# Small matmuls of two gated delta blocks woven into the weight products in a fixed order, and one parameter vector read as one row

## The chip, the cores and the metric

The kernel runs on one core of a Trainium2 chip. The metric is the device time of one execution in microseconds (us). TensorE (PE) multiplies, with its weight loads (PEld) overlapping; VectorE (DVE), ScalarE (ACT) and GpSimd (POOL) do elementwise work; SyncE (SP) and ACT issue the DMAs that matter here, each on a queue of its own.

## The reference

A four-layer hybrid model runs over a prompt of 256 tokens and eight samples of eight tokens, 320 rows of 1024 columns in all, in float32. Each layer is a half feed-forward, a mixer and another half feed-forward. The mixer is a gated delta rule (gdn) in layers 0 and 3, a chunked MLP in one, a state-space mixer (ssd) in one. The gdn mixer:

```python
def gdn_mixer(h, conv_buf, s0, w_in, conv_w, a_log, dt_bias, norm_w, w_out):
    qkv, gate, a_in, b_in = jnp.split(h @ w_in, ...)
    qkv, new_buf = causal_dwconv(qkv, conv_buf, conv_w)
    q, k, v = jnp.split(jax.nn.silu(qkv), [D_QK_A, 2 * D_QK_A], axis=-1)
    q, k = l2norm(q) * (DK_A ** -0.5), l2norm(k)
    g = -jnp.exp(a_log) * jax.nn.softplus(a_in + dt_bias)
    beta = jax.nn.sigmoid(b_in)
    o, s_new = gated_delta_chunked(q, k, v, g, beta, s0)
    o = rms_norm(o, norm_w) * jax.nn.silu(gate)
    return o @ w_out, (new_buf, s_new)
```

There are 8 heads of 128 columns. `gated_delta_chunked` works in chunks: a triangular 128x128 system per head and chunk, made of k·kᵀ, decays from the running sum of g, and beta, is inverted, and the chunk's outputs and the next state follow from it. The ssd mixer has a per-head skip weight, `ssd_d` (32 numbers), by which x is scaled and added to its output.

## The kernel before, in words

Activations stand transposed: 8 tiles of 128 features by 320 rows, each split in a high and a low part (`xhi`, `xlo`). Weights come from HBM in units of 512 KB (`raw`, L133, SP's queue), are split by ACT (`hi`, L134) and DVE (`lo`, L135), and each 128x128 weight block makes three matmuls of 320 columns (hi·hi, lo·hi, hi·lo; L160 to L162). These are called weight products below. The rest of a layer waits for little else than them.

In a gdn block (`gdn_core`, about 267 to 537 us and 2633 to 2903 us of the span) the input projection is done in pairs of heads: k, q, v and the gate g for four head pairs, 16 pairs of column blocks, each 48 weight products. Between and among them stand the chains, one for each head pair, over five 128x128 systems (two heads by two chunks, and the samples):

- `gdn_decay`: after the narrow a/b product, DVE works out softplus and g; PE makes running sums of g (L626 to L660), from which come the decays `Gm`.
- k, q, v pairs are evacuated (`cb`, L538, L539), convolved (one ACT row and three DVE taps, L546) and go through silu.
- `invert(q)`: U and Uq = k·kᵀ and k·qᵀ (L738), a DVE sequence to `L` (L763), a mask product (L768), a loop of 30 small GpSimd operations on `X` (L777, L778), `Dt` (L782), transposes (L786), and three levels of block products with copies between them (L792 to L824).
- `recur(q)`: solve (L860), products with the state (L853 to L868), the sample states (`across`, L898), the norm of the output (L910, L511 on GpSimd, L912), its transposes (L915), then the new sample states: matmuls (L933), DVE updates of `S` (L938), and a store to HBM (L940, SP's queue).

`GDN_ORDER` says between which parts of the chains each pair of products is written; a scheduler then sets the order on every engine by its own costs, with what is ready first. A matmul that waits holds those behind it on PE. `oT`, the gdn output, is split into `g_hi` (L335) and `g_lo` (L336) before the output projection; the memory that `g_hi` takes is free only when the last store of `S` has landed. `psm` is a PSUM pair for the weight products, `psx` and `psy` are sets of three for the chains.

The parameters of a mixer are fetched during the feed-forward before it (`prep_...`). `prep_ssd` reads `ssd_d` into `Dc` (128 partitions by 16), even heads in the upper 64 partitions, odd ones in the lower:

```python
Dc = p.tile([128, 16], F32, name="Dc")
for h in range(2):
    nc.scalar.dma_start(Dc[64 * h:64 * h + 64, :], d['ssd_d'][j].rearrange("(m h) -> h m", h=2)[h].partition_broadcast(64))
```

Of the kernel before, what the change touches and what calls it, by code (L numbers as in the profile page):

```python
# [15 lines left out]
KD = 8  # L16
# [59 lines left out]
GDN_ORDER = "k0 q0 v0,k1 q1,v1 k2,q2,v2,k3 q3,v3,g0,g2,g3 g1"  # L76
# [5 lines left out]
class Trunk:  # L82
    def __init__(self, tc, d, ctx):
# [14 lines left out]
        self.hold, self.homes = [], []  # L98
# [432 lines left out]
    def conv_tile(self, p, ps, ci, prm, cvo):  # L531

        nc = self.nc
        cb = p.tile([128, CB + 8], F32, tag="cb", name="cb", bufs=2)
# [7 lines left out]
                              cb[:, 256:355].rearrange("p (b c) -> p b c", c=11)[:, :, 0:3])  # L542
        y = p.tile([128, CB], F32, tag="cy", name="cy", bufs=2)
# [45 lines left out]
    def gdn_decay(self, t, ab, prep):  # L589
# [34 lines left out]
        g2 = g.rearrange("q p u -> q (p u)")  # L624
        ps, pg = self.psx(), self.psx()
# [47 lines left out]
        return beta, eG, neG, kdc, gt, gts, Gm, last, later  # L673
# [11 lines left out]
    def gdn_core(self, p, j, w_in, prep, cvo):  # L685
        nc, d = self.nc, self.d
        V, A, G, PE = nc.vector, nc.scalar, nc.gpsimd, nc.tensor
        mm = PE.matmul
# [12 lines left out]
        def project(kind, q):  # L701
            if kind == 'k':
# [3 lines left out]
            c0 = {'k': 1024, 'q': 0, 'v': 2048}[kind] + q * 256  # L706
            for h, ps in enumerate(self.pair(w_in, c0)):
                y = self.conv_tile(p, ps, c0 // 128 + h, prm, cvo)
                op, os_ = {'k': (kqp[h][:, :, 0, :], kqs[:, 0]), 'q': (kqp[h][:, :, 1, :], kqs[:, 1]), 'v': (vp[h], vs)}[kind]
                i = A.activation(op, y[:, :TP].rearrange("p (b n) -> p b n", b=2), AF.Silu)  # L710
                if q == 0 and kind != 'k':
                    self.behind(last, i)
                ys = y[:, 259:347].rearrange("p (k j c) -> p k j c", k=2, c=11)[:, :, :, 0:8]
                A.activation(self.rows(os_)[:, h], ys, AF.Silu)
                if kind != 'v':
                    A.activation(EE[q % 3][:, 'kq'.index(kind), 24:].rearrange("p (j k h t) -> p h k j t", j=4, k=2, h=2)[:, h, :, :, 0:8], ys, AF.Silu)

        def gate(q):
            for h, ps in enumerate(self.pair(w_in, 3072 + q * 256)):
                z = t([128, T], "zs", 2)  # L720
                V.tensor_tensor(z, ps, self.r, op=ALU.mult)
                if q in done:
                    A.activation(z, z, AF.Silu)
                    V.tensor_tensor(oT[:, 2 * q + h, :], oT[:, 2 * q + h, :], z, op=ALU.mult)
                else:
                    A.activation(oT[:, 2 * q + h, :], z, AF.Silu)
            gated.append(q)

        def invert(q, fill):
# [4 lines left out]
            U, Uq = t([128, 5, 128], "U"), t([128, 5, 128], "Uq", 2)  # L734
            for a, b in ((0, 2), (2, 4), (4, 5)):
# [25 lines left out]
            for lo, n, w in ((0, 8, 15), (8, 7, 7)):  # L761
# [3 lines left out]
                                d16[:, None, lo:lo + n, None].to_broadcast([128, 5, n, w]), op=ALU.mult)  # L765
            for a, b in ((0, 512), (512, 845)):
# [12 lines left out]
            for f, *a in fill:  # L779
                f(*a)  # L780
# [4 lines left out]
            for u in range(4):  # L785
                PE.transpose(ps[:, u * 128:(u + 1) * 128], Dt[:, u, :], self.ident)  # L786
            A.activation(Dn, ps.rearrange("p (u n) -> p u n", u=4), AF.Copy)
            for u0 in range(0, 4, 2):
                us = slice(u0, u0 + 2)
# [42 lines left out]

        def recur(q, kd, cc, sq, Uq, Dt, S):

            kqp, kqs, vp, vs = tiles.pop(q)
            qu = [kqp[0][:, 0, 1], kqp[0][:, 1, 1], kqp[1][:, 0, 1], kqp[1][:, 1, 1], kqs[:, 1]]
            vu = [vp[0][:, 0], vp[0][:, 1], vp[1][:, 0], vp[1][:, 1], vs]
            R, qss, oss, oe = t([128, 5, 128], "R"), t([128, 5], "qss", 2), t([128, 5], "oss", 2), t([128, 5], "oe", 2)
            for a, b in ((0, 4), (4, 5)):
                ps = self.psx()  # L840
                for u in range(a, b):
                    PE.transpose(ps[:, (u - a) * 128:(u - a + 1) * 128], vu[u], self.ident)
                for u in range(a, b):
                    A.activation(R[:, u], ps[:, (u - a) * 128:(u - a + 1) * 128], AF.Copy, scale=sq[:, u:u + 1])
            vn, o = t([128, 5, 128], "vn"), t([128, 5, 128], "o")
            Sp = t([128, 2, 128], "Sp")
            for b in range(2):
                if b == 1:
                    ps = self.psx()
                    for h in range(2):  # L850
                        for a in range(2):
                            c = (2 * h + a) * 128
                            mm(ps[:, c:c + 128], lhsT=kqp[h][:, 1, a, :], rhs=Sp[:, h], start=True, stop=True)  # L853
                    for h in range(2):
                        u = 2 * h + 1
                        V.scalar_tensor_tensor(R[:, u], ps[:, h * 256:h * 256 + 128], neG[:, q, u:u + 1], R[:, u], op0=ALU.mult, op1=ALU.add)
# [605 lines left out]
```

## Time and profile before

| | us |
|---|---|
| median of 3 runs | 3199.25 (3196.7 to 3200.08) |
| the profiled execution's own time | 3193.62 |
| span of the profiled execution | 3191.8 |
| PE busy, of the span | 3033.1 (95%) |
| DVE / ACT / POOL busy | 1965.6 / 1534.5 / 527.8 |
| mean granted PE clock | 0.966 |

The profiled execution is 5.6 us below the median of the runs. "Busy" is summed over the span; the granted clock is 1.00 where TensorE runs at 2.4 GHz and 0.50 where it runs at 1.2 GHz. Tile names in the rows are those of the program, `out<-in`; L and a number is a line of the kernel before.

### The profile page before, as it was taken

Reading aid. Unit: us, or ns where it says so; the run is one execution under the profiler, and the core shown is the slowest. Engines: PE = TensorE matmul, PEld = TensorE weight load, DVE = VectorE, ACT = ScalarE, POOL = GpSimd, SP = SyncE. Lnnn points to the kernel's source line nnn. Section 1 sums busy time; section 2 is a strip of 40 time slices with the busy share of each in tenths; the row PEclk is TensorE's granted clock in tenths of the full one; section 3 lists DMA queues with packets and bytes.
Section 4 is the critical chain, followed back from the end, with each engine's and each line's share of the span. In section 5 each row is a group of like instructions: output and inputs, shape, how many; then the busy total and the mean of one; then the engine's idle time right before and its main releaser. Section 6 shows DMA issues by size and latency. Waiting matters only on the chain.

```text
span 3191.8 us, 52917 instructions
## 1 busy us (share of the span) xinstructions
PE 3033.1 (95%) x20851; PEld 2907.4 (91%) x20851; DVE 1965.6 (62%) x3365; ACT 1534.5 (48%) x2739; POOL 527.8 (17%) x794
## 2 busy tenths in 40 slices
PE   8998899999999989999899888999999997999998
PEld 8998778999999989999899777799999997778998
DVE  5556775655655675664554787766646647766653
ACT  4445555544444535444444554454444445646443
POOL 1002431000000041001000356510010013331001
PEclk9999898999999999999999989999999998999999
DMA  5444233444444434444444355434444443333543
GB/s 171 148 148 115 82 103 113 138 149 148 148 152 146 146 114 131 150 148 139 123 148 146 103 156 171 139 124 151 148 139 150 143 149 92 90 115 99 158 143 106
DMA packets 464112, 429.28 MB, mean 134 GB/s; under 512 B 20548, under 2 KB 459836, under 8 KB 463800
## 3 DMA queue, kind: packets, MB, share of 16 engines
q1 hardware_dynamic: 446276, 410.58, 42.1%
q10 hardware_dynamic: 17588, 15.33, 1.7%
q8 instruction: 164, 2.69, 0.3%
q14 instruction: 84, 0.69, 0.1%
HBM read 404.06 MB, written 21.79 MB: 133 GB/s over the span
## 4 chain that ended last, share of the span: by engine, by line
PE 84%; DVE 7%; POOL 3%; issue 2%; ACT 2%; DMA 1%; ACTq 0%; SPq 0%; DVEq 0%; POOLq 0%
PE psm L160 14%; PE psm L162 14%; PE psm L161 13%; PE psx L160 11%; PE psx L161 10%; PE psx L162 10%; DVE cy L546 2%; PE psx L933 1%; DMA raw<-ffn_w_in 1%; PE psy L310 1%; PE psy L160 1%; PE psy L162 1%; PE psy L161 1%; ACT hi L134 1%; POOL X L778 1%
## 5 line engine op out<-in xcount | busy, mean ns | idle before, releaser
L135 DVE TENSOR_TENSOR lo<-raw,hi 128x1024 fp32r<-128x1024 f32 x712 | 857.3, 1205 | 800.6 <-ACT hi L134 799.8
L134 ACT ACTIVATE hi<-raw 128x1024 fp32r<-128x1024 f32 x712 | 737.9, 1038 | 854.0 <-PE psm L161 412.8
L160 PE MATMUL psm<-xhi,hi 128*128 128x320 f32 x2328 | 749.1, 322 | 21.4 <-DVE cb L539 17.0
L162 PE MATMUL psm<-xhi,lo 128*128 128x320 f32 x2328 | 740.5, 318 | 1.1 <-DVE lo L135 1.1
L161 PE MATMUL psm<-xlo,hi 128*128 128x320 f32 x2328 | 738.3, 317 | 0.0
L160 PEld LDWEIGHTS psm<-xhi,hi 128*128 128x128 f32 x2328 | 451.0, 194 | 33.0 <-issue 17.9
L162 PEld LDWEIGHTS psm<-xhi,lo 128*128 128x128 f32 x2328 | 450.2, 193 | 9.1 <-issue 5.9
L161 PEld LDWEIGHTS psm<-xlo,hi 128*128 128x128 f32 x2328 | 451.0, 194 | 6.7 <-issue 5.3
L291 POOL TENSOR_TENSOR sqa<-sqa,sq 128x320 f32<-128x320 f32 x90 | 132.5, 1472 | 1836.8 <-ACT sq L288 1831.6
L160 PE MATMUL psx<-xhi,hi 128*128 128x320 f32 x1336 | 414.6, 310 | 0.0
L162 PE MATMUL psx<-xhi,lo 128*128 128x320 f32 x1336 | 413.4, 310 | 0.4 <-DVE lo L135 0.4
L161 PE MATMUL psx<-xlo,hi 128*128 128x320 f32 x1336 | 413.7, 310 | 0.0
L162 PEld LDWEIGHTS psx<-xhi,lo 128*128 128x128 f32 x1336 | 251.3, 188 | 0.7 <-DVE lo L135 0.7
L161 PEld LDWEIGHTS psx<-xlo,hi 128*128 128x128 f32 x1336 | 251.4, 188 | 0.0
L160 PEld LDWEIGHTS psx<-xhi,hi 128*128 128x128 f32 x1336 | 251.4, 188 | 0.0
L161 PE MATMUL psx<-h_lo,hi 128*128 128x320 f32 x704 | 217.6, 309 | 0.0
L162 PE MATMUL psx<-h_hi,lo 128*128 128x320 f32 x704 | 217.5, 309 | 0.0
L161 PE MATMUL psm<-h_lo,hi 128*128 128x320 f32 x704 | 217.4, 309 | 0.0
L160 PE MATMUL psm<-h_hi,hi 128*128 128x320 f32 x704 | 217.3, 309 | 0.0
L162 PE MATMUL psm<-h_hi,lo 128*128 128x320 f32 x704 | 217.3, 309 | 0.0
L160 PE MATMUL psx<-h_hi,hi 128*128 128x320 f32 x704 | 217.3, 309 | 0.0
L335 ACT ACTIVATE h_hi<-us 128x320 fp32r<-128x320 f32 x176 | 81.9, 469 | 165.6 <-DVE us L482 163.6
(542 smaller groups left out, 5244.9 us busy)
## 6 DMA issues: line engine op xcount, KB each, us to landing
raw<-ffn_w_in SPq DMA_DIRECT2D x352, 512.0 KB
raw<-ffn_w_out SPq DMA_DIRECT2D x160, 512.0 KB
raw<-gdn_w_in SPq DMA_DIRECT2D x64, 512.0 KB
raw<-ssd_w_in SPq DMA_DIRECT2D x40, 512.0 KB
raw<-cmlp_w_in SPq DMA_DIRECT2D x32, 512.0 KB
raw<-ffn_w_out SPq DMA_DIRECT2D x32, 256.0 KB
S<-state_gdn SPq DMA_DIRECT2D x16, 512.0 KB
gdn_state_s<-S SPq DMA_DIRECT2D x16, 512.0 KB
```

The lines of the kernel that those rows point to most:

```text
L134: a = nc.scalar.activation(hi, raw, AF.Copy)
L135: v = nc.vector.tensor_tensor(lo, raw, hi.bitcast(F32), op=ALU.subtract)
L160: first = mm(ps, lhsT=w[0], rhs=xhi, start=start, stop=False)
L161: mm(ps, lhsT=w[0], rhs=xlo, start=False, stop=False)
L162: return first, mm(ps, lhsT=w[1], rhs=xhi, start=False, stop=stop)
L291: self.lastadd = (engine or self.nc.gpsimd).tensor_tensor(acc, acc, sq, op=ALU.add)
L310: sums.append(nc.tensor.matmul(ps[:, T + b:T + b + 1], lhsT=s[:, c:c + 128], rhs=self.ones[:, 0:1], start=i == 0, stop=i == len(parts) - 1))
L335: nc.scalar.activation(hi[:, j, :], h, AF.Copy)
L546: nc.vector.scalar_tensor_tensor(y[:, :CL], cb[:, t:t + CL], prm[:, ci, 24 + t:25 + t], y[:, :CL], op0=ALU.mult, op1=ALU.add)
L778: G.tensor_tensor(X[:, :, i + 1:], X[:, :, i + 1:], tmp[:, :, :n], op=ALU.add)
L933: mm(ps, lhsT=kd[32 * i:32 * i + 32, 4], rhs=vE[32 * i:32 * i + 32], start=True, stop=True)
```

## The change

In the gdn blocks every matmul and transpose of `gdn_core` is kept in the order in which the program writes it (`self.pin`, `mm`, `turn`), and the program writes them in steps. `products` yields after every six weight products, so that the 13 pairs other than the first three make 104 steps. `invert` and `recur` of a head pair are one generator, `chain(q)`, cut by `yield` into 36 pieces; after each six weight products every running chain advances by one piece. Chain q starts at step `GDN_START[q]`: 14, 34, 54, 77. So the inversion of a head pair runs while the recurrence of the one before is still under way. The decay is a generator of the same kind: nine empty pieces stand between the a/b transposes and the running sums of g. What is left of the chains when the products end runs by itself (`while chains: step()`); of the last chain, which starts at step 77, these are pieces 27 to 35.

Besides: `conv_tile` is cut into evacuation (`conv_in`, five `cb` buffers in place of two) and taps; the first pairs are all evacuated before the taps; v's transposes and q's norm move from `recur` into `invert`; R and U have two buffers; one `EE` tile for three; the gates are told by head. `prep_ssd` reads `ssd_d` as one contiguous row to all 128 partitions, and two GpSimd copies make `Dc` from it.

```diff
-GDN_ORDER = "k0 q0 v0,k1 q1,v1 k2,q2,v2,k3 q3,v3,g0,g2,g3 g1"
+GDN_ORDER = "k1 q1 v1 k2 q2 v2 v3 k3 q3 g0 g1 g2 g3"
+GDN_START = (14, 34, 54, 77)
...
+    def mm(self, *a, **k):
+        i = self.nc.tensor.matmul(*a, **k)
+        return self.tc.keep_in_program_order(i) if self.pin else i
...
         g2 = g.rearrange("q p u -> q (p u)")
+        for _ in range(9):
+            yield
         ps, pg = self.psx(), self.psx()
...
+        def products(kind, q):
+            pss = [self.psm()[:, :T] for _ in range(2)]
+            for k0, ws in self.blocks(w_in, {'k': 1024, 'q': 0, 'v': 2048, 'g': 3072}[kind] + q * 256, 256, KD):
+                for h, ps in enumerate(pss):
+                    for i in range(0, len(ws), 2):
+                        self.mmblock(ps, k0 + i, ws[i:i + 2], h, self.xhi, self.xlo)
+                        yield
+                    if k0 + len(ws) == KD:
+                        if kind == 'g':
+                            gate(q, h, ps)
+                        else:
+                            put(kind, q, h, take(kind, q, h, ps))
...
                 V.tensor_tensor(Uq[:, a:b], pv[:, :, 1], Gm[:, q, a:b], op=ALU.mult)
+            yield
...
+            for _ in range(5):
+                yield
             for a, b in ((0, 512), (512, 845)):
                 ps = self.psy()
                 mm(ps[:, :b - a], lhsT=cst[:, C_B16:C_B16 + 128], rhs=Lf[:, a:b], start=True, stop=True)
...
+        def step():
+            for q, g in list(chains.items()):
+                if next(g, chains) is chains:
+                    del chains[q]
...
+        chains['d'] = prelude()
+        for w in GDN_ORDER.split():
+            for _ in products(w[0], int(w[1])):
+                if n in GDN_START:
+                    chains[GDN_START.index(n)] = chain(GDN_START.index(n))
+                step()
+                n += 1
+        while chains:
+            step()
+        self.pin = False
...
-        Dc = p.tile([128, 16], F32, name="Dc")
-        for h in range(2):
-            nc.scalar.dma_start(Dc[64 * h:64 * h + 64, :], d['ssd_d'][j].rearrange("(m h) -> h m", h=2)[h].partition_broadcast(64))
+        Dh, Dc = self.bcast(p, d['ssd_d'][j], 32, "Dh"), p.tile([128, 16], F32, name="Dc")
...
+        for h in range(2):
+            nc.gpsimd.tensor_copy(Dc[64 * h:64 * h + 64], Dh[64 * h:64 * h + 64].rearrange("p (m h) -> p h m", h=2)[:, h])
```

**DVE at the decay.** The rows of DVE in the first gdn block that lead up to `gu`, from which g is made (`sp_q` is the softplus polynomial, `cy` a convolution tap, `lo` a weight split). Before:

```order
L135 TENSOR_TENSOR lo<-raw,hi 128x1024
L504 SCALAR_TENSOR_TENSOR sp_q<-sp_q,sp_w 128x24
L546 SCALAR_TENSOR_TENSOR cy<-cb,cprm,cy 128x344
L504 SCALAR_TENSOR_TENSOR sp_q<-sp_q,sp_w 128x24
L546 SCALAR_TENSOR_TENSOR cy<-cb,cprm,cy 128x344
L504 SCALAR_TENSOR_TENSOR sp_q<-sp_q,sp_w 128x24
L546 SCALAR_TENSOR_TENSOR cy<-cb,cprm,cy 128x344
L505 SCALAR_TENSOR_TENSOR sp_q<-sp_q,sp_z 128x24
L546 SCALAR_TENSOR_TENSOR cy<-cb,cprm,cy 128x344
L506 SCALAR_TENSOR_TENSOR gu<-am,sp_q 128x24
```

After the change (L546 is now L566, L135 is L146):

```order
L146 TENSOR_TENSOR lo<-raw,hi 128x1024
L566 SCALAR_TENSOR_TENSOR cy<-cb,cprm,cy 128x344 x6
L515 SCALAR_TENSOR_TENSOR sp_q<-sp_q,sp_w 128x24
L146 TENSOR_TENSOR lo<-raw,hi 128x1024
L566 SCALAR_TENSOR_TENSOR cy<-cb,cprm,cy 128x344
L515 SCALAR_TENSOR_TENSOR sp_q<-sp_q,sp_w 128x24
L566 SCALAR_TENSOR_TENSOR cy<-cb,cprm,cy 128x344 x2
L515 SCALAR_TENSOR_TENSOR sp_q<-sp_q,sp_w 128x24
L566 SCALAR_TENSOR_TENSOR cy<-cb,cprm,cy 128x344 x2
L516 SCALAR_TENSOR_TENSOR sp_q<-sp_q,sp_z 128x24
L566 SCALAR_TENSOR_TENSOR cy<-cb,cprm,cy 128x344
L517 SCALAR_TENSOR_TENSOR gu<-am,sp_q 128x24
```

Between the first row that reads the a/b product (`am`) and the last row of g, 20 taps and 4 splits stand now, where 10 taps and 1 split stood.

**PE at the end of the last chain.** The order on PE around the last chain's output transposes (L915, L917) and sample states (L933), before:

```order
L162 MATMUL psm<-xhi,lo 128x320
L915 MATMUL psx<-cst,o 128x128 x4
L917 MATMUL psx<-cst,o 128x128
L933 MATMUL psx<-R,kd 128x512 x4
L160 MATMUL psm<-xhi,hi 128x320
L161 MATMUL psm<-xlo,hi 128x320
L162 MATMUL psm<-xhi,lo 128x320
L160 MATMUL psm<-xhi,hi 128x320
```

From the first of these weight products on, 36 of them stand before the convolution states' transposes (`cvo`) and the first matmul of the output projection (`g_hi`):

```order
L160 MATMUL psm<-xhi,hi 128x320
L161 MATMUL psm<-xlo,hi 128x320
L162 MATMUL psm<-xhi,lo 128x320
L555 MATMUL psx<-cst,cvo 27x128 x12
L160 MATMUL psm<-g_hi,hi 128x320 x2
L161 MATMUL psm<-g_lo,hi 128x320
L162 MATMUL psm<-g_hi,lo 128x320
```

After the change (all through the helpers at L113 and L117) the last weight product stands two rows ahead of this piece; from piece 27 of the last chain on the order is:

```order
L113 MATMUL psx<-Sp,kqp 128x128 x4
L113 MATMUL psx<-vn,Uq 128x128
L113 MATMUL psx<-R,Dt 128x128 x2
L113 MATMUL psx<-vn,kd 128x128
L113 MATMUL psx<-vn,Uq 128x128
L113 MATMUL psx<-vn,kd 128x128
L113 MATMUL psx<-vn,Uq 128x128
L113 MATMUL psx<-R,kd 128x512 x2
L117 MATMUL psx<-cst,o 128x128 x5
L113 MATMUL psx<-R,kd 128x512 x2
L575 MATMUL psx<-cst,cvo 27x128 x12
L113 MATMUL psm<-g_hi,hi 128x320
```

Between the chain's last pieces and the output projection no weight product is left.

**ACT's DMA queue at `ssd_d`.** The issues on ACT's queue, in the feed-forward ahead of the ssd mixer, before:

```order
L563 DMA dtb<-ssd_dt_bias 128x32
L1084 DMA Dc<-ssd_d 64x16x1 x2
L522 DMA crow<-state_ssd_conv 24x512
L326 ACTIVATE xhi<-xT,nw 128x320
L288 ACTIVATE sq<-xT 128x320
L326 ACTIVATE xhi<-xT,nw 128x320
```

and after, where `Dh` is a row of 32 numbers for each of 128 partitions:

```order
L583 DMA dtb<-ssd_dt_bias 128x32
L583 DMA Dh<-ssd_d 128x32
L533 DMA crow<-state_ssd_conv 24x512
L337 ACTIVATE xhi<-xT,nw 128x320
L299 ACTIVATE sq<-xT 128x320
L337 ACTIVATE xhi<-xT,nw 128x320
```

The place in the queue is the same; one load of 128 rows of 32 stands for two of 64 partitions by 16 single numbers.

## Rows read from the trace of the kernel before

**Rows 1.** The page, part 1: busy time, share of the span, instructions.
```profile
PE 3033.1 (95%) x20851; PEld 2907.4 (91%) x20851; DVE 1965.6 (62%) x3365; ACT 1534.5 (48%) x2739; POOL 527.8 (17%) x794
```

**Rows 2.** Windows: us, each engine's busy time (instructions), granted clock, DMA share, GB/s.
```profile
286.00:545.00 259.00, 226.26 (x1636) 190.97 (x1635) 175.75 (x437) 143.24 (x397) 81.97 (x208) 0.87 0.34 95
545.00:1000.00 455.00, 453.65 (x3106) 452.46 (x3104) 274.42 (x412) 214.67 (x324) 26.59 (x25) 1.00 0.47 146
2651.00:2910.00 259.00, 223.90 (x1642) 189.44 (x1641) 175.32 (x438) 142.95 (x397) 81.96 (x208) 0.89 0.33 96
```

**Rows 3.** Waits, 286 to 545 us: us in total, times, longest.
```profile
PE psy L786 <- DVE Dt L782: 8.5, 1, 8.5
PE psx L915 <- DVE o L912: 8.2, 4, 3.1
PE psx L626 <- DVE cb L539: 6.8, 1, 6.8
PE psy L768 <- DVE L L763: 3.0, 3, 1.9
PE psm L160 <- DVE cb L539: 2.2, 1, 2.2
```

**Rows 4.** Windows: one at half clock, three of nine such stretches, their sum.
```profile
526.20:530.20 4.00, 4.00 (x16) 4.00 (x16) 2.39 (x7) 2.14 (x4) 0.00 (x0) 0.50 0.49 149
...
298.30:308.50 10.20, 7.76 (x32) 7.05 (x33) 4.87 (x25) 4.62 (x12) 1.26 (x6) 0.50 0.13 44
...
523.60:530.40 6.80, 6.80 (x21) 4.75 (x19) 4.89 (x17) 2.34 (x5) 0.00 (x0) 0.50 0.52 166
537.20:540.60 3.40, 2.97 (x12) 2.85 (x12) 3.40 (x10) 2.99 (x8) 0.00 (x0) 0.50 0.89 276
sum 64.80, PE 56.29 PEld 42.67 DVE 39.51 ACT 21.67 POOL 27.04; mean PE 6.25 PEld 4.74 DVE 4.39 ACT 2.41 POOL 3.00
```

**Rows 5.** Waits, 1505 to 1560 us, PE's and SP's queue's.
```profile
PE psy L315 <- POOL rc L313: 12.9, 1, 12.9
...
SPq L133 <- DMA Dc<-ssd_d: 13.6, 1, 13.6
```

**Rows 6.** Timeline, ACT and its queue: start, us; [idle time, releaser].
```profile
1515.93 0.68 ACTq L1084 DMA_DIRECT2D Dc<-ssd_d  x1
...
1540.94 1.06 ACT L134 ACTIVATE hi<-raw 128x1024 fp32r<-128x1024 f32 x1 [16.28 <-DMA raw<-ffn_w_in]
```

**Rows 7.** DMA queues with packets, 1518 to 1535 us: packets, MB, share.
```profile
q10 hardware_dynamic: 1810, 0.01, 4.7%
```

**Rows 8.** Windows, 1520 to 1540 us.
```profile
1520.00:1530.00 10.00, 9.46 (x65) 9.20 (x64) 6.53 (x12) 3.82 (x8) 0.00 (x0) 1.00 0.05 0
1530.00:1540.00 10.00, 4.84 (x35) 4.58 (x33) 0.00 (x0) 0.00 (x0) 0.00 (x0) 0.87 0.26 75
```

**Rows 9.** Timeline, DVE, 287 to 301 us.
```profile
290.56 2.03 DVE L546 SCALAR_TENSOR_TENSOR cy<-cb,cprm,cy 128x344 f32<-128x344 f32 x4
...
295.12 1.21 DVE L135 TENSOR_TENSOR lo<-raw,hi 128x1024 fp32r<-128x1024 f32 x1
```

**Rows 10.** Timeline, PE, 300 to 378 us.
```profile
300.74 0.59 PE L626 MATMUL psx<-g,cst 128*128 128x20 f32 x2 [6.82 <-DVE cb L539]
...
310.66 1.67 PE L738 MATMUL psy<-kqp 128*128 128x256 f32 x7
...
359.66 1.89 PE L738 MATMUL psy<-kqp 128*128 128x256 f32 x8
...
376.81 2.08 PE L768 MATMUL psy<-L,cst 128*128 128x512 f32 x2 [1.86 <-DVE L L763]
```

**Rows 11.** Timeline, SP's queue, 392 to 404 us: state stores, next state loads.
```profile
394.17 1.01 SPq L940 DMA_DIRECT2D gdn_state_s<-S  x2
...
400.72 1.08 SPq L830 DMA_DIRECT2D S<-state_gdn  x2
```

**Rows 12.** Waits, 524 to 546 us.
```profile
PE psm L160 <- ACT g_hi L335: 1.9, 1, 1.9
```

More of the change, by code (lines that the diff above doesn't have):

```diff
@@ L672, in later @@
             exps(1, 4)
-        return beta, eG, neG, kdc, gt, gts, Gm, last, later
+        return beta, eG, neG, kdc, gt, gts, Gm, later
     @staticmethod
@@ L687, in gdn_core @@
         V, A, G, PE = nc.vector, nc.scalar, nc.gpsimd, nc.tensor
-        mm = PE.matmul
+        mm = self.mm
         cst = self.cst
@@ L705, in project @@
             kqp, kqs, vp, vs = tiles[q]
[L706 to L729, printed above, removed]
+            y = self.conv_taps(p, cb, {'k': 8, 'q': 0, 'v': 16}[kind] + 2 * q + h, prm)
@@ new lines, in recur @@
+            outs += [(h, self.seqs(oT[:, 2 * q + h, TP:T])[:, k], self.rows(pt[:, 0:128])[:, h, k]) for h in range(2) for k in range(2)]
+            for h, out, src in outs:
+                if (q, h) in gated:
+                    V.scalar_tensor_tensor(out, src, gnw, out, op0=ALU.mult, op1=ALU.mult)
+                else:
+                    A.activation(out, src, AF.Copy, scale=gnw)
+            done.append(q)
+            for i in (2, 3):
+                yield
+                states(i)
@@ L939, in recur, with chain @@
             for h in range(2):
                 nc.sync.dma_start(d['gdn_state_s'][j, :, 2 * q + h].rearrange("b d e -> d b e"), S[:, h])
-        tiles, gated, done, add = {}, [], [], self.lastadd
+        def chain(q):
+            inv = yield from invert(q)
+            yield from recur(q, *inv, load(q))
+        tiles, gated, done, add = {}, set(), [], self.lastadd
         self.open(w_in, [(1024, 256), (4096, 16), (0, 256)], 2048, narrow)
-        beta, eG, neG, kdc, gt, gts, Gm, last, later = self.gdn_decay(t, self.opened.pop(4096)[0], prep)
@@ L945, in gdn_core @@
-        EE = [t([128, 2, 536], f"ee{i}") for i in range(3)]
-        for i in range(3):
-            self.behind(add, G.memset(EE[i], 0.0))
+        self.pin = True
+        EE = t([128, 2, 536], "ee")
+        self.behind(add, G.memset(EE, 0.0))
         oT = self.cp.tile([128, KD, T], F32, tag="z", name="oT")
-        slots = [[(gate, int(w[1])) if w[0] == 'g' else (project, w[0], int(w[1])) for w in ws.split()] for ws in GDN_ORDER.split(",")]
-        def run(ws):
-            for f, *a in ws:
-                f(*a)
@@ L955, in gdn_core, with prelude @@
-        run(slots[0])
-        inv = invert(0, slots[1])
-        run(slots[2])
-        later()
-        for q in range(4):
-            S = load(q)
-            recur(q, *inv, S)
-            if q < 3:
-                inv = invert(q + 1, slots[3 + 2 * q])
-                run(slots[4 + 2 * q])
-        run(slots[9])
+        got, chains, n = [], {}, 0
+        decay = self.gdn_decay(t, self.opened.pop(4096)[0], prep)
+        next(decay)
+        def prelude():
+            got.extend((yield from decay))
+            yield
+            got[-1]()
@@ new lines, in step @@
+        def step():
+            for q, g in list(chains.items()):
+                if next(g, chains) is chains:
+                    del chains[q]
+        first = {kind: self.opened.pop(c0) for kind, c0 in (('k', 1024), ('q', 0), ('v', 2048))}
+        cbs = {(kind, h): take(kind, 0, h, first[kind][h]) for kind, h in (('v', 1), ('k', 1), ('v', 0), ('q', 0), ('q', 1))}
+        put('k', 0, 1, cbs['k', 1])
+        put('k', 0, 0, take('k', 0, 0, first['k'][0]))
+        for kind in 'qv':
+            for h in range(2):
+                put(kind, 0, h, cbs[kind, h])
```

210 lines of the change are left out of this document (129 added, 81 removed).

## The prediction

> **What bounds the kernel now.** Read the page's busy times first: PE is busy 95% of the span [rows 1], so time can come back only where PE stands still or runs slowly. Then put stretches beside each other by windows [rows 2]. A feed-forward stretch, 545 to 1000 us, has PE busy 453.7 of 455 us at full clock with 3106 matmuls, 0.146 us each: nothing to gain. The first gdn block, 286 to 545 us, has 226.3 of 259 us, clock 0.87; the second is alike (223.9, 0.89). So PE stands still 33 us per block and runs slowly in part of the rest. No other engine is full there: DVE is busy 175.8 of 259 us (68%).
>
> The chain of waits on PE in the block names the places [rows 3]: `Dt` after the GpSimd loop on X, 8.5 us once; the output norm, 8.2 us in four; the decay's g, 6.8 us; `L`, 3.0 us; a PSUM bank still being evacuated, 2.2 us.
>
> The granted clock is the second loss. Nine stretches of the first block, 64.8 us together, have clock 0.50, that is 1.2 GHz in place of 2.4, and PE is busy in 56.3 of them [rows 4]; they lie around and just after those waits. In one of them 16 weight products start in 4.0 us, 0.25 us each against 0.146 [rows 2, 4]. If all busy time there were lost at that rate, 42% of 56.3, it would be 24 us; the small matmuls of the chains are paced less by the clock, so I take 20 us.
>
> A third place lies far from the gdn blocks. In the feed-forward ahead of the ssd mixer PE stands 12.9 us for `rc`, and SP's queue waits 13.6 us on `Dc<-ssd_d` [rows 5]. Follow it back: the two `ssd_d` loads are issued from 1515.93 us; ACT then waits 16.3 us for a raw weight unit, until 1540.94 [rows 6]. In the 17 us between, the only packets on any queue are 1810 of ACT's queue, with 0.01 MB [rows 7]; the stretch 1520 to 1530 us moved 0 GB/s, and PE is down to 4.8 us busy in the next ten [rows 8]. The loads in single numbers (64 partitions by 16, twice: 2048 pieces) hold up the weights.
>
> **The change part by part.** *ssd_d.* The 2048 pieces become 128 rows. What was issued next moves by the difference, some 19 us by 1810 pieces in 17 us; the same rate gives 128 rows 1.2 us. The raw unit then lands before PE wants it. Back come the 12.9 us, and about 1 us of half clock after it (the stretch 1530 to 1540 us ends at 0.87 [rows 8]). I take 14 us; the bounds are 10 (the next unit is late by a few us in its own right) and 16 (the whole ACT wait). The two GpSimd copies are hidden by an engine that is busy 17% of the span [rows 1], and Dc isn't read before the ssd mixer.
>
> *Start of a gdn block.* DVE must reach g. Ten taps and three splits more stand ahead of it. A tap costs 0.51 us (2.03 for four), a split 1.21 [rows 9]: 5.1 + 3.6 = 8.7 us later. The first chain's U, at 310.7 us before [rows 10], is then at about 321 (a few taps more behind g). But by then 14 steps of six weight products are done, 84 where 48 were: (84 - 48) x 0.146 = 5.3 us of work ahead. Net 5 us lost. PE's wait for g grows from 6.8 to about 13 us.
>
> *The middle.* The weave puts weight products between every two pieces, so the waits for Dt, the norm, L and the bank can go: 8.5 + 8.2 + 3.0 + 2.2 = 21.9 us. With them goes the half clock that is not at the block's two ends: 64.8 less 10.2, 6.8 and 3.4 is 44.4 us [rows 4], which as a share of 64.8 is 0.685 of the 20 us, 13.7.
>
> *New waits in the order.* A piece that isn't ready holds all weight products behind it. Length of a step: PE's busy 226 us less 20 for the clock is 206; the some 690 weight products in it take 101; the other 105, in four chains and the decay, are about 25 a chain. Chains start 20 steps apart, so 20 steps last 20 x 6 x 0.146 + 25 = 42.5 us, 2.1 us each. L comes six pieces after U: 12.8 us. Before, it came 17.2 us after U in the second chain, 1.9 of them PE's wait [rows 10]. So PE waits 1 to 4 us there for each chain; the X loop and the copies between the block products have steps enough or one each. I take 8 us a block, between 0 (DVE's queue is in better order than before) and 13, and 4 us of half clock after them (0 to 6). DVE's work, 175.8 us, is not less.
>
> *The end.* The last chain's pieces 27 to 35 run with no weight product beside them, and `g_hi` waits for the landing of the last store. From the second store's issue (394.17 plus 1.01) to the next load, which waits for that memory, were 5.5 us [rows 11]; before, 36 weight products (5.3 us) lay over this and left 1.9 us [rows 12]. With the norm (a third to a quarter of 8.2 us) and the steps of the state update that is some 11 us idle, 1.9 and a norm wait of about 1 less: 8 us lost. The switch between large and small matmuls happens at every step now; between 0 and 5 us, I take 3.
>
> Sum for a block: +5 - 21.9 - 13.7 + 8 + 4 + 8 + 3 = -7.6; two blocks -15, with ssd_d -29 us. From the profiled execution's 3193.6 that is 3165. That execution lies 5.6 us below the median of the runs, so I predict 3170.
>
> **The rivals.**
> *The weave covers nearly all.* No new waits, no half clock after them, no cost of switching (-7.6 - 15 = -22.6), the start and half of the end hidden too (-9): -31 a block, 3199 - 62 - 14 = 3123. For it speaks that PE has 100 us of weight products to lay over at most 33 us of waits; against it, that none is left at the end.
>
> *The fixed order costs more than it hides.* Twelve pieces between X and the last state depend on the piece before through a copy on ACT or DVE; if each waits half a us in four chains that is 24 us, and 8 us of half clock, 32 in place of 12. A block then gives +12.4, and the sum is +25 - 14 = +11: 3210. It decides from 27 us of such waits and clock a block on. For it: DVE is the nearest engine to full, 175.8 of about 250 us, and the waits for L show it late already [rows 3]; against it: a wait lengthens the step, and so gives the next pieces time. The Trainium skill (TensorE: Matmul & The Clock Gate, section on the array's 16 sub-arrays) says that matmuls start in program order, that only weight loads are pulled ahead, and that VectorE and ScalarE take their queues strictly in order. By that rule a late piece costs PE its whole lateness, which is this rival's case; the 8.5 us wait agrees, with weight products left to do.
>
> *ssd_d gives nothing.* If the queues shared the DMA engines fairly, raw units would pass beside the small pieces, and the stall would have another cause and stay: 3199 - 15 = 3184. The rows speak against it: no packet of SP's queue in 17 us [rows 7]. The Trainium skill (DMA: Bandwidth & Descriptors, section Queues, rings and completion order) has each DMA engine take turns among its queues, packet by packet. By that rule the raw unit would not have been held; the trace does not agree, with 0 GB/s.
>
> *The gdn blocks lose what ssd_d gains:* waits and clock of 23 to 27 us in place of 12, near 3196.
>
> **How the numbers follow.** Chances: the forecast 0.47, covering nearly all 0.20, fixed order too dear 0.13, ssd_d nothing 0.08, break-even 0.12. The forecast's own range: with waits, clock and switching at nothing -22.6 a block, at their highest +1.4; with ssd_d 3140 to 3188. What a measurement can tell from no change is about 0.2%, 6.4 us. Faster: 0.47 + 0.20 + 0.08 = 0.75; same 0.12; slower 0.13. The range of 8 in 10 reaches from the covering case, 3120, to break-even with a little loss, 3202.
>
> **What would show it.** After the change, ACT's wait for a raw unit near 1525 us and PE's for `rc` should be under 2 us. In the gdn blocks PE's wait for g should be about 13 us, the waits for Dt and the norm gone from the middle, waits for L of some us left, and at the end about 11 us idle before the first `g_hi` matmul. The windows 286 to 545 us should show clock above 0.92. The prediction is wrong if PE's waits in the middle exceed 20 us a block, or if DVE turns out to be the bound there.

## The result and the profile after

| kernel | us, median (runs) | ratio to before, 95% interval |
|---|---|---|
| before, same chip | 3199.66 (4) | |
| changed | 3219.5 (4, 3217.26 to 3222.15) | 1.0064 (1.0047 to 1.0082) |

The change makes the kernel 20 us slower. The forecast was 3170 us (3120 to 3202) with 0.75 for faster; 0.13 stood on slower, the rival of a fixed order that costs more than it hides, priced at 3210.

The two gdn blocks, from the first a/b matmul to the first matmul of the output projection (columns as in [rows 2]), before:

```profile
267.80:536.80 269.00, 236.69 (x1720) 200.56 (x1718) 184.62 (x454) 147.10 (x403) 86.51 (x215) 0.89 0.34 97
2633.80:2902.30 268.50, 233.79 (x1721) 198.48 (x1718) 184.45 (x455) 147.12 (x403) 86.56 (x215) 0.90 0.34 97
```

Windows of the changed kernel: the same two blocks, and 20 us of the feed-forward ahead of the ssd mixer, from 4.1 us after the `ssd_d` load is issued, as in [rows 8]:

```profile
266.80:553.30 286.50, 233.41 (x1720) 198.14 (x1717) 189.57 (x463) 143.77 (x389) 79.65 (x213) 0.88 0.34 94
2638.90:2925.10 286.20, 234.45 (x1720) 199.23 (x1718) 189.44 (x463) 143.81 (x389) 79.56 (x213) 0.87 0.33 94
1538.40:1548.40 10.00, 10.00 (x70) 10.00 (x69) 8.48 (x14) 6.32 (x10) 2.03 (x2) 1.00 0.66 183
1548.40:1558.40 10.00, 10.00 (x74) 9.77 (x73) 6.73 (x14) 6.30 (x10) 1.71 (x1) 1.00 0.49 151
```

The blocks last 286.5 and 286.2 us, where the same two marks stood 269.0 and 268.5 us apart before. In the first, PE is busy 233.4 us and stands still 53.1 us (before: 236.7 and 32.3). So 17.5 us more are 20.8 us more of idle time and 3.3 us less of busy time. Clock 0.88 and 0.87 are a little below before's 0.89 and 0.90.

The lower two rows answer to [rows 8]: 183 GB/s where there were 0, PE busy 10.0 of 10 us twice where it was 9.5 and 4.8. PE's wait for `rc`, 12.9 us in [rows 5], is gone. The whole profiled span grew by 23.6 us, 3191.8 to 3215.4; the blocks' 17.5 and 17.7 with ssd_d's 12.9 taken off make 22.3 of it.

ACT and its queue at the `ssd_d` load, timeline of the changed kernel:

```profile
1534.30 0.45 ACTq L583 DMA_DIRECT2D Dh<-ssd_d  x1
1534.77 0.42 ACTq L533 DMA_DIRECT2D crow<-state_ssd_conv  x1
...
1542.34 1.06 ACT L145 ACTIVATE hi<-raw 128x1024 fp32r<-128x1024 f32 x1 [0.51 <-DMA raw<-ffn_w_in]
```

One issue of 0.45 us, and the next raw unit that ACT waits for comes after 0.5 us, not after 16.3 [rows 6].

Waits of PE in the first block of the changed kernel (us in total, times, longest):

```profile
PE psx L113 <- DVE o L971: 12.4, 2, 6.7
PE psx L113 <- DVE g L644: 9.5, 1, 9.5
PE psm L113 <- DVE kk L790: 6.7, 1, 6.7
PE psy L117 <- DVE Dt L840: 5.2, 1, 5.2
PE psm L113 <- ACT g_hi L346: 4.3, 1, 4.3
PE psx L117 <- DVE o L978: 3.7, 1, 3.7
PE psx L113 <- ACT o L957: 2.1, 2, 1.6
PE psy L113 <- DVE Dn L862: 1.8, 3, 0.7
PE psx L113 <- DVE R L956: 1.7, 4, 0.6
PE psm L113 <- DVE sp_w L512: 1.5, 1, 1.5
```

Against [rows 3]: Dt fell from 8.5 to 5.2, the norm from 8.2 to 3.7 (the end's alone), g rose from 6.8 to 9.5 with 1.5 for `sp_w`, a bank (behind `kk`) from 2.2 to 6.7. The bank's wait stands for an evacuation (`cb`) that DVE does behind 15 rows of the other three head pairs' decays. No wait for `L` is left. New is the largest, 12.4 us in two waits for `o` (L971), the addition that frees a PSUM bank of the chain: the next state matmul (L933, now L113) needs that bank. Why `o` is late stands in DVE's timeline just before:

```profile
384.28 0.35 DVE L956 SCALAR_TENSOR_TENSOR R<-psx,neG,R 128x128 f32<-128x128 f32 x1 [0.63 <-ACT o L957]
385.85 0.29 DVE L961 TENSOR_TENSOR o<-o,psx 128x128 f32<-128x128 f32 x1 [1.23 <-PE psx L113]
393.14 0.83 DVE L840 TENSOR_TENSOR Dt<-X,cst 128x640 f32<-128x640 f32 x1 [7.00 <-POOL X L818]
394.00 0.24 DVE L814 COPY X<-cst 128x80 f32<-128x80 f32 x1
394.15 0.60 DVE L968 SCALAR_TENSOR_TENSOR Sp<-Sp,gt,psx 128x128 f32<-128x128 f32 x2
394.67 0.41 DVE L971 TENSOR_TENSOR o<-o,psx 128x256 f32<-128x256 f32 x1
```

DVE stands still 7.0 us for Dt (L840), which waits for the GpSimd loop on X. Behind Dt in DVE's queue stand the two updates of Sp (L968) and `o` (L971). PE has made their inputs when its wait begins, at 389.5 us; `o` runs at 394.67. Dt belongs to the next chain. In the program it is written seven steps after `o`; only PE is kept in program order, and the scheduler has put Dt ahead on DVE. The same happens with the next chain, 7.6 us.

### The profile page after: what moved, and what is told of

It reads as the page before. It is cut to its first block, busy times and chain, and to the rows that moved or that the text cites. A ratio compares the mean times of both kernels' runs of the same rounds, so it can differ in the third digit from the quotient of the medians.

```text
span 3215.4 us, 52868 instructions
## 1 busy us (share of the span) xinstructions
PE 3035.1 (94%) x20851; PEld 2910.0 (91%) x20851; DVE 1971.1 (61%) x3373; ACT 1528.3 (48%) x2711; POOL 505.4 (16%) x792
## 3 DMA queue, kind: packets, MB, share of 16 engines
q1 hardware_dynamic: 446276, 410.58, 41.9%
## 4 chain that ended last, share of the span: by engine, by line
PE 82%; DVE 8%; POOL 4%; ACT 3%; issue 2%; DMA 2%; ACTq 0%; SPq 0%; DVEq 0%; POOLq 0%
PE psm L113 39%; PE psx L113 34%; PE psy L113 3%; DVE cy L566 2%; POOL tmp L817 1%; POOL X L818 1%; DVE lo L146 1%; ACT hi L145 1%; PE psy L321 1%; PE psx L1463 1%; DVE Gm L1365 1%; PE psy L326 1%; PE psx L1459 0%; DVE vt L1146 0%; POOL sqa L302 0%
## 5 line engine op out<-in xcount | busy, mean ns | idle before, releaser
L146 DVE TENSOR_TENSOR lo<-raw,hi 128x1024 fp32r<-128x1024 f32 x712 | 859.7, 1208 | 800.8 <-ACT hi L145 799.8
L113 PE MATMUL psm<-xhi,hi 128*128 128x320 f32 x2328 | 760.3, 327 | 37.8 <-DVE cb L555 15.2
L113 PE MATMUL psm<-xhi,lo 128*128 128x320 f32 x2328 | 734.7, 316 | 1.1 <-DVE lo L146 1.1
L113 PE MATMUL psm<-xlo,hi 128*128 128x320 f32 x2328 | 734.0, 315 | 0.0
L113 PEld LDWEIGHTS psm<-xhi,hi 128*128 128x128 f32 x2328 | 451.0, 194 | 69.2 <-issue 48.7
L113 PEld LDWEIGHTS psm<-xlo,hi 128*128 128x128 f32 x2328 | 451.1, 194 | 1.4
L113 PEld LDWEIGHTS psm<-xhi,lo 128*128 128x128 f32 x2328 | 449.6, 193 | 2.3 <-DVE lo L146 1.6
L113 PE MATMUL psx<-xhi,hi 128*128 128x320 f32 x1336 | 414.2, 310 | 0.0
L113 PE MATMUL psx<-xhi,lo 128*128 128x320 f32 x1336 | 413.0, 309 | 0.4 <-DVE lo L146 0.4
L113 PE MATMUL psx<-xlo,hi 128*128 128x320 f32 x1336 | 413.2, 309 | 0.0
L302 POOL TENSOR_TENSOR sqa<-sqa,sq 128x320 f32<-128x320 f32 x90 | 119.1, 1323 | 1827.2 <-ACT sq L299 1821.5
L113 PEld LDWEIGHTS psx<-xhi,lo 128*128 128x128 f32 x1336 | 250.9, 188 | 0.7 <-DVE lo L146 0.7
L113 PEld LDWEIGHTS psx<-xlo,hi 128*128 128x128 f32 x1336 | 251.1, 188 | 0.0
L113 PEld LDWEIGHTS psx<-xhi,hi 128*128 128x128 f32 x1336 | 251.1, 188 | 0.0
L113 PE MATMUL psx<-h_lo,hi 128*128 128x320 f32 x704 | 217.7, 309 | 0.0
L113 PE MATMUL psx<-h_hi,lo 128*128 128x320 f32 x704 | 217.5, 309 | 0.0
L113 PE MATMUL psm<-h_lo,hi 128*128 128x320 f32 x704 | 217.5, 309 | 0.0
L113 PE MATMUL psm<-h_hi,lo 128*128 128x320 f32 x704 | 217.4, 309 | 0.0
L113 PE MATMUL psm<-h_hi,hi 128*128 128x320 f32 x704 | 217.4, 309 | 0.0
L113 PE MATMUL psx<-h_hi,hi 128*128 128x320 f32 x704 | 217.3, 309 | 0.0
```

The source lines that it names most:

```text
L113: i = self.nc.tensor.matmul(*a, **k)
L146: v = nc.vector.tensor_tensor(lo, raw, hi.bitcast(F32), op=ALU.subtract)
L302: self.lastadd = (engine or self.nc.gpsimd).tensor_tensor(acc, acc, sq, op=ALU.add)
```

## The experiments

Two theories at the start: A, DVE's queue is what holds PE, and each place mended gives its wait back; B, the fixed order on PE turns whatever is late in a chain into a wait, and a wait mended returns at the next place. "Block" is the first gdn block between the same marks, "idle" the sum of PE's gaps in it (the one before the first matmul of the output projection too), "half" the time at clock 0.50 in it, all worked out from each profiled execution.

| run | edit | us | ratio to before (95%) | block | idle | half |
|---|---|---|---|---|---|---|
| before | | | | 269.0 | 32.3 | 61.4 |
| changed | | 3219.5 | 1.0064 (1.0047 to 1.0082) | 286.5 | 53.1 | 65.9 |
| e1 | before + ssd_d row | 3180.5 | 0.9954 (0.9940 to 0.9969) | 267.7 | 35.0 | 51.2 |
| e2 | changed, old ssd_d | 3231.9 | 1.0118 (1.0103 to 1.0133) | 286.8 | 52.9 | 72.5 |
| e3 | changed, PE not pinned | 3205.7 | 1.0027 (1.0016 to 1.0037) | 279.7 | 47.0 | 58.6 |
| e4 | changed, Dt pinned on DVE | 3210.4 | 1.0049 (1.0032 to 1.0067) | 282.8 | 51.5 | 58.9 |
| e5 | e4 + decay early | 3206.5 | 1.0034 (1.0022 to 1.0045) | 282.0 | 45.7 | 75.1 |
| e6 | e4 + half steps in g2, g3 | 3214.8 | 1.0061 (1.0046 to 1.0076) | 283.2 | 46.0 | 64.9 |
| e7 | e4 + other decays late | 3205.1 | 1.0029 (1.0017 to 1.0042) | 280.9 | 45.0 | 62.3 |
| e8 | e4 + e5, e6, e7 | 3203.3 | 1.0018 (1.0006 to 1.0030) | 272.3 | 43.2 | 41.3 |
| e9 | e4, PE not pinned | 3200.4 | 1.0010 (1.0001 to 1.0019) | 275.8 | 41.1 | 58.8 |
| e10 | e4, short loop | 3176.9 | 0.9936 (0.9920 to 0.9951) | 269.5 | 41.9 | 45.3 |
| e11 | e4, one tap | 3173.3 | 0.9922 (0.9904 to 0.9941) | 263.9 | 35.1 | 49.8 |
| e12 | e9 + e5, e7 | 3191.9 | 0.9988 (0.9975 to 1.0001) | 278.5 | 36.7 | 70.2 |
| e13 | e1, short loop | 3161.6 | 0.9885 (0.9863 to 0.9906) | 260.0 | 24.3 | 58.0 |
| e14 | e1, one tap | 3174.1 | 0.9922 (0.9902 to 0.9943) | 266.4 | 31.6 | 58.0 |
| e15 | e12 + closer starts | 3160.3 | 0.9882 (0.9863 to 0.9900) | 254.5 | 27.2 | 29.0 |
| e16 | e15, PE pinned | 3187.0 | 0.9962 (0.9950 to 0.9975) | 270.4 | 39.7 | 55.2 |
| e17 | changed + closer starts | 3211.3 | 1.0041 (1.0026 to 1.0056) | 283.5 | 54.9 | 62.3 |
| e18 | e17, PE not pinned | 3192.9 | 0.9981 (0.9972 to 0.9990) | 274.1 | 47.5 | 49.5 |

The chips differ from batch to batch, so differences between kernels are taken below from the ratios, times 3199 us.

**The two parts apart (e1, e2).** e1 puts the new `prep_ssd` in the kernel before, e2 the old one in the changed kernel.

> The kernel before with the change to ssd_d alone. Both theories: the 12.9 us wait of PE for rc in the feed-forward ahead of the ssd mixer goes, and nothing else moves: 13 us under the kernel before, near 3187. A result within 5 us of the kernel before would say that the stall only hid another wait.

> The changed kernel with the old loads of ssd_d. Both theories: the two gdn blocks each stay 16 to 18 us longer than before and the stall at ssd_d is back: 13 us over the changed kernel, near 3233. If it were under 3225, the two parts would not add.

e1 is 14.7 us faster (10 to 19), e2 38 us slower, that is 17 more than the changed kernel. The two parts add within the intervals, and the loss is the weave's alone.

**Who holds PE: its own order or DVE's (e3, e4, e9).**

```diff
e3, e9: -        self.pin = True
e4, e9:
-            V.tensor_tensor(Dt.rearrange("p u (b i) -> p u b i", b=8), ...)
+            self.tc.keep_in_program_order(V.tensor_tensor(Dt.rearrange("p u (b i) -> p u b i", b=8), ...))
```

> The changed kernel, its matmuls left to the scheduler (pin stays off), the program text otherwise the same. Theory A (DVE's queue: Dt, which waits for the GpSimd loop, stands ahead of the evacuations that PE needs): DVE's order is the scheduler's in both, so the idle times of 7 us of DVE before Dt stay for the most part and PE fills only part of them with weight products: 3200 to 3215. Theory B (the fixed order on PE is what costs): PE's waits fall by half or more, 3165 to 3190.

> The changed kernel with one more instruction kept in program order, Dt on DVE (after the evacuations and state updates written before it). Theory A: the two waits of 5.7 and 6.7 us for o (L971) go in each block, with part of the half clock after them: 25 to 40 us less than the changed kernel, 3180 to 3195. Theory B: PE's next piece waits in its place and the time stays within 6 us of the changed kernel, 3213 to 3225.

e3 gives 12 us back and e4 5, by ratios whose intervals overlap for e4 (its block is 3.7 us shorter). For e3 A's figure holds and B's fails; for e4 A's fails, and the 5 us lie within B's 6 (its median, 3210.4, lies between the two forecasts). PE's waits in e3:

```profile
PE psx L113 <- DVE o L971: 12.8, 2, 6.7
PE psm L113 <- DVE kk L790: 6.8, 1, 6.8
PE psy L117 <- DVE Dt L840: 5.9, 1, 5.9
```

With PE free the waits for `o` are all there: the scheduler put the same matmul there, and DVE stands as before. So Dt's place on DVE makes them. But taking them away (e4) does not shorten the block by as much:

```profile
PE psy L117 <- DVE Dt L841: 11.4, 3, 7.2
PE psx L113 <- DVE g L644: 9.6, 1, 9.6
PE psx L117 <- DVE o L979: 7.0, 3, 4.1
PE psm L113 <- DVE kk L790: 6.5, 1, 6.5
```

The 12.4 us for `o` are gone; Dt rose from 5.2 to 11.4, the norm from 3.7 to 7.0, together 9.5 us. Most of the wait has moved on along the chain.

> The kernel of e4 (Dt kept in program order on DVE) with PE left to the scheduler. If the fixed order on PE and Dt's place on DVE each cost their own waits: the gain of e3 (14 us) and that of e4 (9 us) add, near 3196 and some 5 us more of half clock, 3188 to 3198. If it is one loss seen twice (PE stands because DVE stands): no more than either, 3203 to 3212.

Together they give 17 us (1.0064 to 1.0010): the sum of 12 and 5. 2 us above the forecast for a sum, 3 below that for one loss. The two add within the intervals, and the block is still 7 us longer than before.

**Mending place by place in the fixed order (e5 to e8).** e5 runs the decay's first piece ahead of the convolutions, e7 puts ten empty pieces for one ahead of `later()` (the other three pairs' decays), e6 halves the steps of the last two pairs:

```diff
e5: +        chains['d'] = prelude()
    +        step()
             first = {kind: self.opened.pop(c0) for kind, c0 in ...}
    ...
    -        chains['d'] = prelude()
e6: -                    for i in range(0, len(ws), 2):
    -                        self.mmblock(ps, k0 + i, ws[i:i + 2], h, self.xhi, self.xlo)
    +                    w = 1 if kind == 'g' and q > 1 else 2
    +                    for i in range(0, len(ws), w):
    +                        self.mmblock(ps, k0 + i, ws[i:i + w], h, self.xhi, self.xlo)
e7: -            yield
    +            for _ in range(10):
    +                yield
             got[-1]()
```

> The kernel of e4 (Dt kept in program order) with the decay's first DVE part written ahead of the convolutions: 8 taps and 2 splits stand before g where 20 and 4 stood. Theory A (each wait is what one late row of DVE costs the fixed order on PE, and comes back when it goes): PE's wait of 9.6 us for g falls to 1 to 3 us, 14 to 20 us less than e4, 3190 to 3197. Theory B (DVE's work for the chains is the bound, and a wait taken away returns at the next place): U of the first chain still waits for the taps, the time stays within 6 us of e4, 3204 to 3216.

> The kernel of e4 with steps of three weight products in place of six in the last two pairs, so that there are 120 steps and the last chain ends at step 113. Theory A: the waits behind the products' end (4.1 for the norm, 4.2 for g_hi, some 2 more) go for the most part, 12 to 20 us less than e4, 3190 to 3198. Theory B: they come back as waits inside the last two pairs, whose steps cover half as much each: within 6 us of e4.

> The kernel of e4 with the decays of the other three head pairs (15 rows of DVE that wait for a DMA) written ten pieces later. Theory A: the first chain's L sequence and the evacuation behind which PE waits 6.5 us for a bank come some 6 us earlier, 10 to 15 us less than e4, 3195 to 3200. Theory B: the first chain then waits longer for Dt, within 6 us of e4.

> The three edits of e5, e6 and e7 together on e4. Theory A: the sum of the three, 36 to 50 us less than e4, 3160 to 3175, below the kernel with the ssd_d row alone. Theory B: not under 3190.

Against e4: e5 gives 5 us, e7 6, e6 loses 4, and all three give 10, where A had 36 to 50. The single ones are within the intervals; e8's blocks are 10.5 and 0.6 us shorter. B's figures hold for e5, e6 and e8; e7's 6.4 us lie at the edge of its 6. Idle time does fall, from 51.5 to 43.2, but the places mended held some 20 (9.6, 6.5 and 4.2 of them for g, the bank and g_hi). In e8 the wait for g is gone and the bank's is 1.2 us, and others have grown:

```profile
PE psy L117 <- DVE Dt L842: 14.0, 4, 8.8
PE psm L113 <- DVE cb L555: 6.8, 2, 6.0
PE psy L113 <- ACT hi L145: 3.3, 1, 3.3
```

Dt had 11.4 us in e4, `cb` 1.2, and `hi` none. So A's sum fails here, as B's figure did in e3: neither theory holds alone.

**Is it the chain's length (e10, e11, e13, e14)?** Take work out of the chains, in the fixed order (e10, e11) and in the order of before (e13, e14). `t0` is 3 in the gdn convolutions and 1 elsewhere.

```diff
e10, e13: -            for i in range(15):
          +            for i in range(5):
e11, e14: -        for t in range(1, 4):
          +        for t in range(t0, 4):
```

> The kernel of e4 with 5 of the 15 passes of the GpSimd loop on X; ten passes of the inversion's base are left out, some 6 us of 11 in each chain. Theory L (latency of a chain's serial rows against 2 us steps): the waits for Dt (11.4 us a block) go, 20 to 30 us less than e4, 3180 to 3190. Theory W (DVE's work is the bound): they return at the next place, within 6 us of e4.

> The kernel of e4 with one of three DVE taps in the gdn convolutions; two taps a tile are left out, 24 us of DVE's work in a block. Theory W (DVE's work is the bound): the waits for g, the bank and the norm fall by half or more, 25 to 45 us less than e4, 3165 to 3185. Theory L: only the waits right behind taps fall (g, some 5 us a block), 3195 to 3205.

> The kernel of e1 (the order of before, ssd_d as a row) with 5 of the 15 passes of the GpSimd loop; ten passes of the inversion's base are left out. If the fixed steps made the chain's serial length the limit: less than 20 us under e1 (before has one wait for Dt, 8.5 us a block), 3162 to 3178. If the chains set the time before too: 28 us or more under e1, below 3153.

> The kernel of e1 with one of three DVE taps in the gdn convolutions; two taps a tile are left out. If the fixed steps made it the limit: less than 20 us under e1, 3162 to 3178. If DVE's work set the time before too: 28 us or more under e1, below 3153.

The loop is worth 36 us in the fixed order (1.0049 to 0.9936) and 22 in the old one (0.9954 to 0.9885); the taps 41 us in the fixed order and 10 in the old one (forecast for the old one: under 20, or 28 and more; the loop is just above the first). Neither theory holds alone in the fixed order: e10 gains more than theory L's 20 to 30 us, e11 lies in theory W's 25 to 45, and each theory's figure for the other's piece fails. The expectations put what is left out at 6 us of the loop in each of eight chains and 24 us of taps in each of two blocks, 48 us either way (an estimate); 36 and 41 of them come back. A chain's rows are in series there, the loop's and DVE's. In the old order DVE's taps have room, and the loop less. So DVE became critical in the new order, which it was only in part before; the loop was so before too. The two orders differ in the steps, in PE's fixed order and in e4's edit together, and these runs don't tell which of them did it.

**When the chains start (e12, e15 to e18).**

```diff
-GDN_ORDER = "k1 q1 v1 k2 q2 v2 v3 k3 q3 g0 g1 g2 g3"
-GDN_START = (14, 34, 54, 77)
+GDN_ORDER = "k1 q1 v1 k2 q2 v2 k3 q3 v3 g0 g1 g2 g3"
+GDN_START = (14, 32, 50, 70)
```

> The kernel of e9 with the decay's DVE part written early (e5) and the other decays late (e7): no fixed order on PE, the three places on DVE mended. If the fixed order on PE is what keeps the waits alive: 3165 to 3185, as fast as the kernel with the ssd_d row alone or faster. If the weave itself, with 36 pieces of a chain in steps, is too tight for the chain's latency: 3190 to 3205.

> The kernel of e12 with the chains' starts at 14, 32, 50 and 70 (k3 and q3 ahead of v3), so that the last chain ends with the products. If the late last chain is what is left (its U comes 12 us later than before): 8 to 16 us less than e12, 3175 to 3184. If it is the half clock, which falls on any order with some 30 us of waits: within 6 us of e12, 3186 to 3198.

> The same as e15 with PE kept in program order from the first chain on. If closer starts make each step longer but the chains no shorter, PE's waits grow in the fixed order: 3198 to 3212. If the last chain's tail was the loss: 3180 to 3192.

> The changed kernel with the closer starts (14, 32, 50, 70; k3 and q3 ahead of v3) and nothing else. If the late last chain was the loss: 15 to 30 us less than the changed kernel, 3190 to 3205. If the fixed order on PE meets DVE's waits (for o, the bank and g, each where it is), they stay and the starts give only the end: 3208 to 3218.

> The same with PE left to the scheduler, without the edits on DVE (e15 less those). If the starts and PE's freedom are what made e15 fast: 3160 to 3175. If the edits on DVE are needed too: 3180 to 3195.

e12 takes 7 us off e9, and its 3191.9 lies in the second forecast: mending DVE's places with PE free does not reach e1. e15 is the fastest of all kernels run that leave nothing out: 38 us faster than before and 23 faster than e1. It beat its own forecast by 15 us, so its theory had the way right and the size not. Its waits and its blocks:

```profile
PE psm L113 <- ACT g_hi L346: 5.7, 1, 5.7
PE psx L117 <- DVE o L979: 4.3, 2, 2.5
PE psy L117 <- DVE Dt L841: 3.4, 1, 3.4
PE psy L113 <- ACT kqp L737: 3.4, 1, 3.4
PE psy L113 <- DVE L L801: 3.2, 3, 1.5
```

```profile
270.50:525.00 254.50, 227.32 (x1720) 191.78 (x1718) 187.50 (x461) 146.62 (x394) 88.57 (x213) 0.94 0.37 104
2611.70:2866.60 254.90, 226.73 (x1719) 190.68 (x1717) 187.35 (x460) 146.50 (x394) 88.37 (x213) 0.95 0.36 104
```

No wait is over 5.7 us, and clock is 0.94 to 0.95. The fourth chain's U starts at 442.6 us, where it was 457.2 before and 475.9 in the changed kernel (172, 189 and 209 us into the block). With PE pinned (e16) everything else is the same, and 26 us go:

```profile
PE psy L117 <- DVE Dt L841: 17.0, 4, 8.9
PE psm L113 <- DVE cb L555: 8.2, 3, 6.0
PE psm L113 <- ACT g_hi L346: 5.2, 1, 5.2
```

Dt waits four times for 17.0 us, once for each chain: PE comes to Dt's transposes at a set place and can't pass them. By its own forecast e16's 3187.0 lies in the range for the last chain's tail as the loss; set beside e15 it shows that the fixed order is a loss too. e17 and e18 each lie in the second range of theirs, in which the starts alone are not enough. The starts alone give 7 us to the changed kernel (e17) and 15 to it with PE free (e3 to e18); the edits on DVE then give 32 more (e18 to e15).

## Why the prediction was wrong

- **ssd_d: right.** 14 us forecast, 12.9 in the trace, 14.7 (10 to 19) in e1. The rival by which queues share fairly is out: with 128 rows in place of the small pieces the raw units flow, 183 GB/s where there were 0. The turns that the Trainium skill describes (DMA: Bandwidth & Descriptors, section Queues, rings and completion order) did not protect the other queue here.
- **Start: right.** U of the first chain at 320.1 us (forecast 321), with 42 weight products more ahead of it than before (forecast 36: the fifteenth step's six are ahead of it too); waits 9.5 and 1.5 us (forecast 13).
- **End: right.** 9.7 us idle from 526 us on (forecast 11): 3.7 for the norm, 4.3 for `g_hi` and small ones.
- **The middle: the step that failed is "new waits in the order", 8 us a block with bounds 0 and 13.** Without start and end the gaps are 53.1 - 11.1 - 9.7 = 32 us. The sum lists 21.9 us that "can go"; as much and more came back. The waits for L, for which the 8 us were taken, did not come at all; others did. Two things were left out. First, I priced a piece's wait against the step length alone (L after 12.8 us), without asking what stands ahead of each row on DVE now (the bound 0 even supposed a better order there); Dt ahead of `o` is a row of that order, with 12.4 us of waits behind it. Second, I added waits as if they were independent. e4 to e8 show that they are not: of a wait mended at one place, most is paid at others in the fixed order.
- **The half clock: 13.7 us were to go, 4 to come back.** 65.9 us at half clock for 61.4 before: nothing went. But it is not what made the block longer. The stretches at clock 0.50 in the first block of the changed kernel, their sum:

```profile
sum 65.90, PE 47.41 PEld 35.36 DVE 45.10 ACT 25.29 POOL 14.32; mean PE 5.93 PEld 4.42 DVE 5.64 ACT 3.16 POOL 1.79
```

  Before, PE was busy in 53.3 of 61.4 us (the sum in [rows 4] without its last stretch, which lies behind the block). Busy time at half clock counted by half, PE's rows come to 210.0 us before and 209.7 after: 5.9 us less of it are 3.0 of the 3.3 us by which PE's busy time fell. No run shows the 3 us for switching between large and small matmuls, and these sums leave no room for it. The price of 20 us was low too: in both traces the output transposes start 0.21 us apart at clock 0.50 and 0.11 at 1.00, weight products 0.27 and 0.15, so the small matmuls are paced no less by the clock, and 53.3 busy us cost about 27.
- **The sum.** It had idle time at -0.9 us a block (5 - 21.9 + 8 + 8) and busy time at -6.7 (-13.7 + 4 + 3); measured are +20.8 and -3.3. These 21.7 and 3.4 us are the 25 between -7.6 and +17.5.
- **The rival had the right sign and a part of the mechanism.** It named the order on PE and DVE's load, and 24 us of waits and 8 of clock, 3210 us in all for 3219.5 measured. That this is near is in part luck, since its place was wrong: the copies between pieces (Dn, R, vn) cost 1 to 2 us each group, not 24. The rule that it weighed (the Trainium skill, TensorE: Matmul & The Clock Gate, section The mechanism, on packing small matmuls: matmuls start and end in their order) agrees: in e16 PE waits at Dt's transposes with weight products left.

What caused the 17.5 us is shown in part. The fixed order on PE costs 12 us over both blocks on the changed kernel (e3) and 26 where the rest is mended (e15 to e16). The late starts cost 15 us with PE free (e3 to e18), and Dt's place on DVE with the two decay edits 32 (e18 to e15). These are clear of their intervals. Alone on the changed kernel, Dt's place (e4) and the starts (e17) are not: 5 and 7 us in time, 3.7 and 3.0 in the first block. All of them together (e15) take 32 us off a block. How the 17.5 split among them can't be given, since each edit is worth more when the others are made. What else the change does (five `cb` buffers, the first pairs all evacuated ahead of the taps, the moved transposes and norm) was not varied by itself.

## What to carry to other kernels

When one engine's order is fixed by hand, look at the queues of the others that the scheduler still sets: a row there that waits for a slow engine holds everything behind it, and the fixed engine can't go round. Don't add waits of a serial chain as independent gains; take work out of the chain (here ten loop passes, two taps) and see what comes back, in both orders. A load of 2048 single numbers cost 14.7 us here through a queue that it was not on: read parameter vectors as rows.

## What the runs showed of the hardware

The 2048 pieces of the old `ssd_d` loads, 8 KB, held up another queue's 512 KB units. From 1518 to 1535 us no packet of SP's queue moved [rows 7], although it had issued a raw unit early in that stretch, and one more at 1525.27 us:

```profile
1520.45 0.37 SPq L133 DMA_DIRECT2D raw<-ffn_w_in  x1
```

e1 shows the pieces worth 14.7 us. Whether they held the units in the DMA engines or ahead of them was not tried.

The half clock does not follow the idle time alone. e8's two gdn blocks run the same program with 43.2 and 41.8 us of PE gaps, yet one is 8.7 us shorter, with 41.3 us at half clock and not 61.4. The first row is block 1, the second block 2:

```profile
265.50:537.80 272.30, 229.09 (x1720) 194.20 (x1718) 188.86 (x457) 148.66 (x397) 85.56 (x213) 0.92 0.35 97
2623.20:2904.30 281.10, 239.31 (x1721) 200.96 (x1718) 187.61 (x457) 148.94 (x397) 84.49 (x213) 0.89 0.33 94
```

PE is busy 10.2 us longer in the second for the same matmuls: 52.6 us of its busy time there lie at clock 0.50, and 30.4 in the first, and half of that difference is 11.1 us. And e12 against e1, first blocks, idle 36.7 and 35.0 us:

```profile
270.00:548.60 278.60, 241.89 (x1721) 201.86 (x1718) 187.62 (x464) 146.11 (x391) 85.47 (x213) 0.87 0.35 97
```

```profile
266.40:534.10 267.70, 232.75 (x1721) 197.35 (x1718) 184.51 (x454) 146.96 (x403) 86.31 (x215) 0.90 0.35 97
```

Here 70.2 and 51.2 us at half clock go with 278.5 and 267.7 us. How long the gaps were in all does not decide it; what does was not tried and stays open.
